# Key norms by one block-ones product, and small products set apart, in a hybrid RWKV-7 / sparse-attention layer

## The chip, the cores and the metric

The kernel runs on one core of one Trainium2 chip. The metric is device time in microseconds (us). Before the change the median of three runs is 1169.22 us (1169.16 to 1169.35). The profile is one more execution, taken by the hardware profiler.

## The reference

One decoder layer on 512 tokens of width 1024. A combined projection of the normalised input feeds two mixers, RWKV-7 time mixing and sparse attention; their outputs are gated, merged and projected, and a gated MLP with a causal convolution follows. All of it is float32. The change touches the RWKV-7 part:

```python
kk = heads(k * k_k)                       # 16 heads of 64 channels
kk = kk / jnp.maximum(jnp.sqrt(jnp.sum(kk * kk, axis=-1, keepdims=True)), 1e-12)
k = k * (1.0 + (a - 1.0) * k_a)
y = wkv7_scan(r, decay, k, v, -kk, kk * a)
mean = jnp.mean(y, axis=-1, keepdims=True)
var = jnp.mean(jnp.square(y - mean), axis=-1, keepdims=True)
y = ((y - mean) * lax.rsqrt(var + GN_EPS)) * ln_w + ln_b
y = (y + jnp.sum(r * k * r_k, axis=-1, keepdims=True) * v) * g
```

So the keys are divided by their norm in each head, the scan runs over time, and its output is normalised per head, scaled, shifted, joined by a bonus term and multiplied by a gate.

## The kernel before

**Layout.** Channels lie on the 128 partitions and the 512 tokens on the free axis. Sixteen heads make eight pairs, p = 0 to 7, in two groups of four. A projection of one block of 128 columns (`proj_steps`, L302) is 24 TensorE products of 128x512: each weight block is split into a high and a low part in a reduced-precision float32 format, and for each of eight k-tiles three products are made (L306, L307, L308). A product of two such parts is one pass; a product of two plain float32 operands shows as two records in the profile. The split (`split_w`) loads the raw weights, copies them to the high part on ScalarE (L124) and subtracts on GpSimd (L162); three buffers are turned for each of raw, high and low.

**Order.** The program is written as Python generators. `drive` takes one step of a filler (one k-tile of a projection, three products) and lets other generators, the threads, go on at given rates: a `yield` in a thread is a point where filler products come between. A scheduler then sets the order of each engine's instructions; `keep_in_program_order` pins some. Engines run their instructions in that order, and an instruction that waits holds up all those behind it on its engine.

**Stages of the RWKV part.** For each pair: `inputs` projects k, r and v and mixes each with its shifted self; `prep` makes the decay, the key norm and the scaled operands; `couple` makes the products between tokens of a chunk of 64 (L607), transposes (L140), and stores the bonus term (`bvd`, L642). For each group of four pairs, `invert` inverts the triangular blocks on VectorE, and `recur` first completes the inverses by small products of 32x32 (`mt` L705, `mm` L728) and then goes through eight chunks: state times operand (xw, L789), output (y, L760 and L753), solve (L805), state update (xs, L815). Between its chunks it collects the sums of the group norm (`stat1`, `stat2`). `finish` normalises, transposes back, applies ln_w and ln_b, adds the bonus and multiplies by the gate (L880, L881). The pairs 0 to 3 are prepared from 81 to 180 us; the first recurrence lies at 227 to 288 us, with the prep of pair 4 beside it; pairs 5 to 7 and the finish of the first group follow until 385 us; the second recurrence is at 437 to 488 us. From 488 us the scores of the sparse attention run, with the finish of the second group among them.

**The key norm.** In `prep`, Q holds the squares of the scaled keys, channels by tokens. Four products (`pn`, L541) with `sel`, a 128x2 matrix of ones and zeros, use pieces of Q as the stationary operand and give, for 128 tokens each, the sums of the two heads; the result has tokens on the partitions and eight columns. ScalarE takes the root (L543, with a table load ahead of it and one after it for the exponential), VectorE the maximum with 1e-12, a factor 2 and the reciprocal on 128x8. GpSimd spreads these to 128x512 (`nte`, L551; ScalarE L549 for pair 4), and four transposes (`pb`, L140) bring them back to channels by tokens in PSUM. From there VectorE multiplies them into KB (L570) and AR (L572).

**Other lines.** In `recur`, `stat1` subtracts the mean on GpSimd (L773) and squares on ScalarE (L775) right behind it. In `finish`, ScalarE applies ln_w and ln_b out of PSUM (L868, L871), GpSimd adds the loaded bonus (`bvl`, L857, L872), and VectorE multiplies by the gate product. At the end of the MLP, `post` multiplies the second half by its gain (L1363) and adds the two halves of the sum of squares (L1364) before the root and the reciprocal of the last norm.

## Time and profile before

| what | us |
|---|---|
| median of the runs | 1169.22 |
| the profiled execution's own time | 1171.52 |
| its span, first to last instruction | 1169.7 |
| TensorE busy (98%) | 1148.6 |
| VectorE busy (49%) | 574.0 |
| ScalarE busy (50%) | 579.5 |
| GpSimd busy (51%) | 595.2 |

Busy time of TensorE is the time in which at least one product is under way; neighbouring products overlap, so the spacing of their starts, not the duration of one, tells what a product costs. The page also gives the clock that the throttle granted to TensorE, and each view can be cut to a window. "Idle before" names what ended the wait of an engine.

### The profile page before, as it was taken

To read this page: it belongs to the slowest core of one execution; us is meant where nothing else is said; L and a number is where in the kernel's file an instruction comes from. 1 tells how busy PE (TensorE), PEld (TensorE's weight loads), DVE (VectorE), ACT (ScalarE), POOL (GpSimd) and SP (SyncE) were. 2 spreads that over 40 slices of the span, in tenths; PEclk is the share of its full clock that TensorE was granted. 3 is DMA by queue.
4 is the path that set the end of the run, shared out by engine and by line. 5 is a ranking of instruction groups with operands and counts; after the bars stand their busy time and mean duration, and the time that the engine had idled before them with its cause. 6 is when DMAs were issued, how large, how long until landed. Compare 5 with 4: busy or idle time off the path is not lost.

```text
span 1169.7 us, 19903 instructions
## 1 busy us (share of the span) xinstructions
PE 1148.6 (98%) x7418; PEld 927.3 (79%) x7418; DVE 574.0 (49%) x1196; ACT 579.5 (50%) x1149; POOL 595.2 (51%) x537
## 2 busy tenths in 40 slices
PE   9999999999999999999999999999999999999997
PEld 7888888867878887767677778889888888888886
DVE  4236555634456563587798735754443343331103
ACT  6446663534665334477576654534444444443311
POOL 4346654335666452497666635511565556554430
PEclk9999999989999999999999999999999999999999
DMA  7522335311443662225543136641233333334421
GB/s 245 134 65 75 103 99 167 96 64 53 113 125 93 188 198 92 91 60 145 170 149 97 46 97 181 209 156 39 80 99 99 97 94 99 99 97 136 127 64 72
DMA packets 95651, 131.95 MB, mean 113 GB/s; under 512 B 34177, under 2 KB 37057, under 8 KB 95298
## 3 DMA queue, kind: packets, MB, share of 16 engines
q1 hardware_dynamic: 79634, 116.26, 33.1%
q10 hardware_dynamic: 15920, 14.42, 3.9%
q8 instruction: 58, 0.95, 0.3%
q14 instruction: 39, 0.32, 0.1%
HBM read 108.30 MB, written 19.14 MB: 109 GB/s over the span
## 4 chain that ended last, share of the span: by engine, by line
PE 87%; DVE 4%; ACT 3%; POOL 2%; issue 1%; DMA 1%; SPq 0%; DVEq 0%; ACTq 0%; POOLq 0%
PE pu L223 6%; PE pu L221 6%; PE pu L222 6%; PE dn L1317 3%; PE dn L1316 3%; PE dn L1315 3%; PE o L1142 3%; PE pt L140 3%; PE ub L1199 3%; PE ub L1201 2%; PE ub L1200 2%; PE gt L306 2%; PE gt L308 2%; PE gt L307 2%; PE v L306 2%; PE v L308 2%
## 5 line engine op out<-in xcount | busy, mean ns | idle before, releaser
L1095 ACT ACTIVATE p<-p,stt 128x384 f32<-128x384 f32 (+3 forms) x128 | 70.7, 554 | 34.5 <-DVE stt L1093 32.9
L1069 POOL TENSOR_SCALAR p<-p,stt 128x512 f32<-128x512 f32 (+1 forms) x64 | 72.3, 1139 | 25.8 <-DVE stt L1064 15.5
L1457 DVE SCALAR_TENSOR_TENSOR u<-pu,cvec,u 128x511 f32<-128x511 f32 x44 | 33.0, 750 | 101.2 <-ACT u L1456 101.2
L1093 DVE CUSTOM_DVE_ANT_0 p<-s,rh 128x384 f32<-128x384 f32 (+3 forms) x128 | 59.0, 484 | 22.7 <-PE s L1079 18.3
L1463 DVE TENSOR_TENSOR al<-u,ah 128x512 fp32r<-128x512 f32 x22 | 23.8, 1080 | 45.4 <-ACT ah L1462 45.4
L140 PE MATMUL pt<-ident,p 128*128 128x128 f32 x320 | 44.3, 272 | 0.0
L1086 PE MATMUL s<-kst,qs 128*128 128x512 f32 (+1 forms) x128 | 39.2, 396 | 4.4 <-DVE stt L1093 4.1
L1461 POOL TENSOR_TENSOR u<-u,u 128x512 f32<-128x512 f32 x22 | 28.3, 1288 | 27.3 <-DVE u L1458 26.3
L1142 PE MATMUL o<-PT,vt 128*64 128x256 f32 (+3 forms) x256 | 41.5, 443 | 0.0
L140 PEld LDWEIGHTS pt<-ident,p 128*128 128x128 f32 x320 | 37.8, 141 | 4.4 <-issue 0.4
L1069 DVE TENSOR_SCALAR p<-p,stt 128x512 f32<-128x512 f32 (+1 forms) x64 | 35.3, 580 | 0.8
L1456 ACT ACTIVATE u<-pu,cvec 128x512 f32<-128x512 f32 x44 | 33.6, 764 | 3.0 <-PE pu L1419 3.0
L1458 DVE SCALAR_TENSOR_TENSOR u<-pu,cvec,u 128x510 f32<-128x510 f32 x44 | 33.0, 749 | 1.6
L1086 PEld LDWEIGHTS s<-kst,qs 128*128 128x128 f32 x128 | 20.9, 189 | 13.5 <-DVE stt L1093 9.3
L1142 PEld LDWEIGHTS o<-PT,vt 128*64 128x64 f32 x256 | 16.6, 136 | 18.8 <-issue 16.8
L1133 ACT ACTIVATE PT<-pt 128x512 f32<-128x512 f32 x48 | 27.3, 584 | 8.0 <-PE pt L140 7.8
L1363 DVE TENSOR_TENSOR p2tm<-dn,gb 128x512 f32<-128x512 f32 x4 | 2.8, 692 | 51.2 <-ACT p2jl L1361 51.2
L1135 DVE COPY PT<-pt 128x512 f32<-128x512 f32 x32 | 21.7, 678 | 8.4 <-PE pt L140 8.3
L1462 ACT ACTIVATE ah<-u 128x512 fp32r<-128x512 f32 x22 | 13.9, 633 | 22.0 <-POOL u L1461 22.0
L1095 ACT ACTIVATION_READ_ACCUMULATOR p<-p,stt 128x1 f32 x128 | 24.2, 189 | 0.0
L664 DVE TENSOR_TENSOR XP<-XP,TM 128x30 f32<-128x30 f32 (+14 forms) x60 | 20.3, 338 | 2.0
L162 POOL TENSOR_TENSOR up3l<-up30r,up3h 128x512 fp32r<-128x512 f32 x1 | 1.3, 1295 | 38.2 <-ACT up3h L124 38.2
(1755 smaller groups left out, 3953.8 us busy)
## 6 DMA issues: line engine op xcount, KB each, us to landing
gtd<-gt ACTq DMA_DIRECT2D x16, 256.0 KB, 2.2
qs<-qd SPq DMA_DIRECT2D x32, 128.0 KB, 3.3
g<-gtd SPq DMA_DIRECT2D x16, 256.0 KB, 3.2
xt<-in_x_dram SPq DMA_DIRECT2D x4, 512.0 KB, 5.5
bvd<-bv SPq DMA_DIRECT2D x8, 256.0 KB, 2.2
bvl<-bvd SPq DMA_DIRECT2D x8, 256.0 KB, 2.9
oad<-y SPq DMA_DIRECT2D x8, 256.0 KB, 2.5
kst<-kst ACTq DMA_DIRECT2D x16, 128.0 KB, 2.5
```

The source lines that it names most:

```text
L140: return te.transpose(o, i, ident)
L221: te.matmul(p, wh(k), mh(k), start=first and k == 0, stop=False)
L222: te.matmul(p, wh(k), ml(k), start=False, stop=False)
L223: te.matmul(p, wl(k), mh(k), start=False, stop=last and k == n - 1)
L306: te.matmul(p, wh(k), hh[:, k, :], start=k == 0, stop=False)
L308: te.matmul(p, wl(k), hh[:, k, :], start=False, stop=k == KT - 1)
L1069: (po if b else ve).tensor_scalar(o.pe[e, b, k], o.pe[e, b, k], st[e][:, 3, i:i + 1], None, op0=OP.mult)
L1086: m = te.matmul(s_[:, :n], qt, kt[:, x, b, :n], start=x == 0, stop=x == 1)
L1093: ve.tensor_tensor_reduce(sb, parts[b], rh[e][:, (3 - qb) * 128:], -1.0, BIG, OP.add, OP.min, st[e][:, 0, i:i + 1])
L1095: sc.activation(sb, sb, AF.Exp, scale=-1.0, bias=st[e][:, 0, i:i + 1], accum_out=st[e][:, 1, i:i + 1])
L1142: te.matmul(acc[e * 64:e * 64 + 64, j * 128:], vt[:, j, b * 256 + g * 64:b * 256 + g * 64 + 64], m[e][:, c:c + n], start=False, stop=k == ...
L1199: te.matmul(p, wh(k), sh[:, k, :], start=k == 0, stop=False)
```

## The change

The eight parts of the edit, and what each does:

1. **Key norm.** `pb` is now one float32 product of the 128x128 block matrix of ones (`onesr`, already there for the bonus term) with Q: each channel gets the sum of its head. Maximum with 1e-24, root and reciprocal then work in place on 128x512 in PSUM. The factors 2 and -2 become 0.5 and -1 in the two multiplications that read `pb`. The four `sel` products, the spreading and the four transposes are gone.
2. **Weight splits ahead.** While k is projected, the split of r's weights is issued after the sixth of eight k-tiles, and v's while r is projected.
3. **Two more yields in `couple`** ahead of the transposes of v and the products L607.
4. **Bunches in `recur`.** Two yields between each block of `mt` or `mm` products and its copies out of PSUM, so that the two blocks are apart; fewer yields after them. The inner products of y keep the program's order for the first seven chunks.
5. **Squares.** The squaring moves out of `stat1` to a later point of the next chunk, with two buffers.
6. **Finish.** The bonus is loaded straight into y2; VectorE applies ln_w and adds the bonus in one instruction out of PSUM, and adds ln_b as it multiplies by the gate. The ScalarE and GpSimd instructions for this are gone, the low part of g2 is split for 128 columns instead of 256, and the y2 buffers are two.
7. **Buffers.** `gates_` and one `plain_out` use the tag of y2 in place of that of `bvl`.
8. **Last norm.** The 128x1 addition goes ahead of the 128x512 multiplication.

How the order of the engines' instructions moves is shown at three places, of before and then of the change. A row has the line, the operation, output<-inputs and the size; xN counts equal rows that follow each other.

VectorE in the prep of pair 0. Before, from the norms (nt) to the operand AR:
```order
L544 TENSOR_SCALAR nt_918<-nt_918 128x8
L545 RECIPROCAL nt_918<-nt_918 128x8
L563 SCALAR_TENSOR_TENSOR Q_891<-K_643,vec,EC_924 128x512
L561 SCALAR_TENSOR_TENSOR A_937<-pa_901,EN_925 128x512
L565 TENSOR_TENSOR KB_936<-F_905,EN_925 128x8x64
L562 SCALAR_TENSOR_TENSOR A_937<-K_643,vec,A_937 128x512
L331 SCALAR_TENSOR_TENSOR K_874<-k_875,vec,K_874 128x511
L570 TENSOR_TENSOR KB_936<-pb_945,A_937 128x8x64
L572 SCALAR_TENSOR_TENSOR AR_859<-Q_891,pb_945 128x512
```

The change, from the maximum on the product pb to AR:
```order
L547 TENSOR_SCALAR pb_911<-pb_911 128x512
L559 SCALAR_TENSOR_TENSOR A_929<-pa_899,EN_917 128x512
L561 SCALAR_TENSOR_TENSOR Q_889<-K_641,vec,EC_916 128x512
L560 SCALAR_TENSOR_TENSOR A_929<-K_641,vec,A_929 128x512
L563 TENSOR_TENSOR KB_928<-F_903,EN_917 128x8x64
L549 RECIPROCAL pb_911<-pb_911 128x512
L332 SCALAR_TENSOR_TENSOR K_872<-k_873,vec,K_872 128x511
L565 SCALAR_TENSOR_TENSOR KB_928<-pb_911,A_929 128x8x64
L568 SCALAR_TENSOR_TENSOR AR_857<-Q_889,pb_911 128x512
```
The reciprocal is now 128x512 and stands four instructions further back, next ahead of K, KB and AR; KB (L563) stands ahead of it.

TensorE where the first recurrence begins (mt and mm are the products that complete the inverses, gt a projection that fills). Before, around mt and then around mm:
```order
L307 MATMUL gt_2323<-hl,gt04h_2324 128x512
L308 MATMUL gt_2323<-hh,gt04l_2325 128x512
L705 MATMUL mt_2365<-x_2126 32x32 x32
L705 MATMUL mt_2400<-x_2126 32x32 x32
L306 MATMUL gt_2323<-hh,gt04h_2330 128x512
L307 MATMUL gt_2323<-hl,gt04h_2330 128x512
...
L308 MATMUL gt_2323<-hh,gt04l_2331 128x512
L728 MATMUL mm_2455<-TT_870,x_2126 32x32 x32
L140 MATMUL pb_2564<-ident,nte_2354 128x128 x3
L728 MATMUL mm_2490<-TT_870,x_2126 32x32 x32
L140 MATMUL pb_2564<-ident,nte_2354 128x128
L805 MATMUL xw_2552<-LV_869,TT_870 64x64 x4
L805 MATMUL xs_2553<-LV_869,TT_870 64x64 x2
```

The change:
```order
L308 MATMUL gt_2277<-hh,gt04l_2279 128x512
L703 MATMUL mt_2313<-x_2092 32x32 x32
L306 MATMUL gt_2277<-hh,gt04h_2284 128x512
...
L308 MATMUL gt_2277<-hh,gt04l_2285 128x512
L703 MATMUL mt_2354<-x_2092 32x32 x32
L306 MATMUL gt_2277<-hh,gt04h_2284 128x512
...
L308 MATMUL gt_2406<-hh,gt14l_2408 128x512
L306 MATMUL gt_2406<-hh,gt14h_2413 128x512
L727 MATMUL mm_2422<-TT_868,x_2092 32x32 x32
L727 MATMUL mm_2463<-TT_868,x_2092 32x32 x32
L307 MATMUL gt_2406<-hl,gt14h_2413 128x512
```
Six filler products part the two mt blocks, and nineteen stand between mt and mm; the two mm blocks still follow each other, and the transposes into pb are gone.

ScalarE in the first recurrence (UV copies out of xs, YT out of y, SQ squares, v0h high parts of weights). Before, chunks 3 and 4:
```order
L775 ACTIVATE SQ_2755<-YT_2525 128x512
L810 ACTIVATE UV_868<-xs_2725 64x4x64
L764 ACTIVATE YT_2525<-y_2602 128x4x64
L764 ACTIVATE YT_2525<-y_2603 128x4x64
L810 ACTIVATE UV_868<-xs_2786 64x4x64
L124 ACTIVATE v0h_3016<-v01r 128x512
```

The change, chunks 2 to 4:
```order
L814 ACTIVATE UV_866<-xs_2619 64x4x64
L124 ACTIVATE v0h_2863<-v01r 128x512
L779 ACTIVATE SQ_2732<-YT_2511 128x512
L814 ACTIVATE UV_866<-xs_2677 64x4x64
L766 ACTIVATE YT_2511<-y_2554 128x4x64
L766 ACTIVATE YT_2511<-y_2555 128x4x64
L814 ACTIVATE UV_866<-xs_2738 64x4x64
```
The square still stands directly ahead of the UV copy of chunk 3 (in the change xs_2677, before xs_2725); the copies of weights around it moved.

```diff
@@ -299,13 +299,15 @@
...
 
-    def proj_steps(blk, name, p):
-        wh, wl = split_w(a["wf"][blk], name)
+    def proj_steps(blk, name, p, w=None, ahead=None):
+        wh, wl = w or split_w(a["wf"][blk], name)
         wh, wl = wslice(wh), wslice(wl)
...
             te.matmul(p, wl(k), hh[:, k, :], start=False, stop=k == KT - 1)
+            if ahead is not None and k == 5:
+                ahead()
             yield
...
@@ -486,18 +487,23 @@
...
     def inputs(p, o):
+        w = {}
+
+        def ahead(x):
+            w[x] = split_w(a["wf"]["rkv".index(x) + 3 + 3 * p], f"{x}{p}")
+
         K = o.K = rw.tile([128, S], F32, tag="K", name=f"K{p}", bufs=2)
         pk = pj(f"k{p}")
-        yield from proj_steps(4 + 3 * p, f"k{p}", pk)
+        yield from proj_steps(4 + 3 * p, f"k{p}", pk, None, lambda: ahead("r"))
         shift(pk, K, 8 + p)
...
         pr = pj(f"r{p}")
-        yield from proj_steps(3 + 3 * p, f"r{p}", pr)
+        yield from proj_steps(3 + 3 * p, f"r{p}", pr, w["r"], lambda: ahead("v"))
         shift(pr, R, p)
...
         pv = pj(f"v{p}")
-        yield from proj_steps(5 + 3 * p, f"v{p}", pv)
+        yield from proj_steps(5 + 3 * p, f"v{p}", pv, w["v"])
         shift(pv, VW[:, 64:], 16 + p)
...
@@ -536,19 +542,11 @@
...
         yield
-        pn = (pz if p == GP else py)(f"pn{p}")
-        for t in range(4):
-            te.matmul(pn[:, 2 * t:2 * t + 2], Q[:, t * 128:(t + 1) * 128], sel, start=True, stop=True)
-        nt = rw.tile([128, 8], F32, tag="nt", name=f"nt{p}", bufs=2)
-        sc.activation(nt, pn[:, :8], AF.Sqrt)
-        ve.tensor_scalar(nt, nt, 1e-12, 2.0, op0=OP.max, op1=OP.mult)
-        ve.reciprocal(nt, nt)
-        nte = rw.tile([128, 8, 64], F32, tag="T", name=f"nte{p}", bufs=NT)
-        nb = nt[:, :, None].to_broadcast([128, 8, 64])
-        if p == GP:
-            sc.activation(nte, nb, AF.Copy)
-        else:
-            po.tensor_copy(nte, nb)
+        pb = pz(f"pb{p}")
+        te.matmul(pb, onesr.bitcast(F32), Q, start=True, stop=True)
+        ve.tensor_scalar(pb, pb, 1e-24, None, op0=OP.max)
+        sc.activation(pb, pb, AF.Sqrt)
+        ve.reciprocal(pb, pb)
         EC = rw.tile([128, 8, 65], F32, tag="EC", name=f"EC{p}", bufs=1)
...
@@ -564,12 +562,10 @@
...
         yield
-        pb = pz(f"pb{p}")
-        for t in range(4):
-            tr(pb[:, t * 128:(t + 1) * 128], nte[:, 2 * t:2 * t + 2].rearrange("p a b -> p (a b)"), ident)
-        ve.tensor_tensor(KB[:, :, 0, :], pb.rearrange(c8, t=64), A.rearrange(c8, t=64), op=OP.mult)
+        ve.scalar_tensor_tensor(KB[:, :, 0, :], pb.rearrange(c8, t=64), 0.5, A.rearrange(c8, t=64), op0=OP.mult,
+                                op1=OP.mult)
         o.Q = None if gr else Q
-        ve.scalar_tensor_tensor(gr.AR[p % GP][:, 0, :] if gr else Q, Q, -2.0, pb, op0=OP.mult, op1=OP.mult)
+        ve.scalar_tensor_tensor(gr.AR[p % GP][:, 0, :] if gr else Q, Q, -1.0, pb, op0=OP.mult, op1=OP.mult)
         tc.keep_in_program_order(ve.scalar_tensor_tensor(F, R, vec[:, V_RK + p:V_RK + p + 1], F, op0=OP.mult,
...
@@ -588,6 +584,8 @@
...
         sc.activation(gr.Dc[:, i], EC[:, :, 64], AF.Copy)
+        yield
+        yield
         yield
...
@@ -706,6 +704,8 @@
...
                             tc.keep_in_program_order(m)
+            yield
+            yield
             for h in range(2):
...
@@ -716,8 +716,7 @@
...
             behind(sc.activation(gr.diag[0][lo, :, 0:32], gr.diag[1][lo], AF.Copy))
-        for _ in range(4):
-            yield
+        yield
         for q in range(GP // 2):
...
@@ -727,6 +726,8 @@
...
                                   stop=True)
+            yield
+            yield
             for h in range(2):
...
@@ -734,8 +735,7 @@
...
         YT = gr.YT = rh_.tile([128, 4, GP, 2, 64], F32, tag="XB", name=f"YT{g}", bufs=2)
-        for _ in range(3):
-            yield
+        yield
         hs = [slice(0, 64), slice(64, 128)]
...
@@ -757,8 +757,10 @@
...
                 for i in range(GP):
-                    te.matmul(y[h][hs[(c + i) % 2], i], gr.GS[:, 1 + i, c, h, :], gr.UV[:, c, i, h, :],
-                              start=c == 0, stop=c == 0 or i >= 2)
+                    m = te.matmul(y[h][hs[(c + i) % 2], i], gr.GS[:, 1 + i, c, h, :], gr.UV[:, c, i, h, :],
+                                  start=c == 0, stop=c == 0 or i >= 2)
+                    if c < 7:
+                        tc.keep_in_program_order(m)
             if c % 2:
...
@@ -771,8 +773,10 @@
...
             po.tensor_tensor(Y8, Y8, st[:, 0, a, :, None].to_broadcast([128, 2 * GP, 64]), op=OP.subtract)
-            sq[a] = rh_.tile([128, 2 * GP, 64], F32, tag="TB", name=f"SQ{g}{a}", bufs=1)
-            sc.activation(sq[a], Y8, AF.Square)
+
+        def square(a):
+            sq[a] = rh_.tile([128, 2 * GP, 64], F32, tag="TB", name=f"SQ{g}{a}", bufs=2)
+            sc.activation(sq[a], YT[:, a].rearrange("p i h v -> p (i h) v"), AF.Square)
 
...
@@ -821,11 +825,15 @@
...
                 St = SN
+                if c >= 3 and c % 2:
+                    square((c - 3) // 2)
                 yield
...
                 inner(c)
+        square(2)
         stat2(2, free)
         stat1(3, free)
+        square(3)
 
...
@@ -849,36 +857,38 @@
...
             gh = rh_.tile([128, 256], F32R, tag="gh", name=f"gh{p}", bufs=1)
-            gl = rh_.tile([128, 256], F32R, tag="gl", name=f"gl{p}", bufs=1)
-            split_to(a["g2"][p], gh, gl, f"g2{p}", 256, p=rh_, late=True, tag="TM", bufs=1)
-            po.tensor_copy(gh[64:96, 128:], gl[64:96, 128:].bitcast(F32))
-            yield
-            bvl = rh_.tile([128, S], F32, tag="bvl", name=f"bvl{p}", bufs=1)
-            tc.keep_in_program_order(sy.dma_start(bvl, bvd[p]))
+            gl = rh_.tile([128, 128], F32R, tag="gl", name=f"gl{p}", bufs=1)
+            raw = rh_.tile([128, 256], F32, tag="TM", name=f"g2{p}r", bufs=1)
+            sy.dma_start(raw, a["g2"][p])
+            tc.keep_in_program_order(sc.activation(gh, raw, AF.Copy))
+            po.tensor_tensor(gl, raw[:, :128], gh[:, :128].bitcast(F32), op=OP.subtract)
+            gx = gh[64:96, 128:]
+            po.tensor_tensor(gx, raw[64:96, 128:], gx.bitcast(F32), op=OP.subtract)
+            yield
+            y2 = rh_.tile([128, S], F32, tag="TB", name=f"y2{p}", bufs=2)
+            tc.keep_in_program_order(sy.dma_start(y2, bvd[p]))
             yield
...
                 tr(pt[:, t * 128:(t + 1) * 128], Y8[:, t].rearrange("p h v -> p (h v)"), ident)
-            y2 = rh_.tile([128, S], F32, tag="TB", name=f"y2{p}", bufs=1)
             y2v = y2.rearrange("p (t s u) -> p t s u", s=2, u=64)
...
             if i % 2 == 0:
-                sc.activation(y2, pt, AF.Identity, scale=lnw, bias=lnb)
+                ve.scalar_tensor_tensor(y2, pt, lnw, y2, op0=OP.mult, op1=OP.add)
             else:
                 for x in range(2):
-                    sc.activation(y2v[:, :, x], ptv[:, :, 1 - x], AF.Identity, scale=lnw, bias=lnb)
-            po.tensor_tensor(y2, y2, bvl, op=OP.add)
+                    ve.scalar_tensor_tensor(y2v[:, :, x], ptv[:, :, 1 - x], lnw, y2v[:, :, x], op0=OP.mult, op1=OP.add)
             yield
...
             te.matmul(pg, gh[:, :128], lg1l, start=False, stop=False)
-            te.matmul(pg, gl[:, :128], lg1h, start=False, stop=False)
+            te.matmul(pg, gl, lg1h, start=False, stop=False)
             te.matmul(pg, gh[:96, 128:], lg2, start=False, stop=True)
-            ve.tensor_tensor(y2, y2, pg, op=OP.mult)
+            ve.scalar_tensor_tensor(y2, y2, lnb, pg, op0=OP.add, op1=OP.mult)
             sy.dma_start(oad[p], y2)
...
@@ -1360,8 +1370,8 @@
...
         tm = p.tile([128, 512], F32, tag=name + "tm", name=f"{name}tm{t}", bufs=3)
+        ve.tensor_tensor(ss[:, 2:3], ss[:, 0:1], ss[:, 1:2], op=OP.add)
         ve.tensor_tensor(tm, acc, gb[:, 512:], op=OP.mult)
-        ve.tensor_tensor(ss[:, 2:3], ss[:, 0:1], ss[:, 1:2], op=OP.add)
         r = rstd_of(ss[:, 2:3], D, f"{name}r{t}", p)
...
```

## The prediction, written before the result

> **What bounds the kernel now.** I read the page's first parts, then the view of TensorE's waits, then windows and timelines of the stages that the change touches.

> The page's busy line, and its chain of waits by engine:
> ```profile
> PE 1148.6 (98%) x7418; PEld 927.3 (79%) x7418; DVE 574.0 (49%) x1196; ACT 579.5 (50%) x1149; POOL 595.2 (51%) x537
> ...
> PE 87%; DVE 4%; ACT 3%; POOL 2%; issue 1%; DMA 1%; SPq 0%; DVEq 0%; ACTq 0%; POOLq 0%
> ```
> TensorE is busy for 98% of the span and holds 87% of the chain; the others are half idle. So time goes only where TensorE issues less, waits less, or runs at a better clock. Its waits (the columns are us in total, times, longest):
> ```profile
> PE s L1086 <- DVE stt L1093: 4.1, 7, 1.3
> PE xs L815 <- ACT UV L810: 2.3, 4, 0.8
> ...
> PE s L1079 <- DVE y L881: 1.3, 1, 1.3
> ...
> PE pg L880 <- POOL gh L854: 0.9, 1, 0.9
> PE r L308 <- POOL r6l L162: 0.6, 1, 0.6
> ```
> The clock is seen in windows (length, busy time of PE, PEld, DVE, ACT, POOL with instructions, granted clock, DMA share, GB/s):
> ```profile
> 229.80:233.20 3.40, 3.40 (x44) 2.85 (x39) 1.47 (x3) 3.32 (x5) 0.00 (x0) 0.50 0.02 5
> ...
> 240.06:246.86 6.80, 6.80 (x20) 4.17 (x18) 2.35 (x4) 1.16 (x4) 4.18 (x3) 0.50 0.38 118
> ...
> 441.45:444.75 3.30, 3.30 (x9) 2.57 (x8) 0.70 (x1) 3.26 (x3) 0.00 (x0) 0.50 0.02 6
> ...
> 488.00:560.00 72.00, 68.58 (x393) 50.60 (x389) 58.50 (x190) 53.09 (x146) 57.61 (x62) 1.00 0.39 110
> ```
> Both recurrences begin with a stretch in which TensorE is busy throughout and has half its clock; elsewhere the clock is nearly full.

> **The change part by part.** All terms are TensorE time.

> *Products of the key norm.* TensorE in the prep of pair 0 (start, duration):
> ```profile
> 83.16 0.40 PE L308 MATMUL k<-hh,k1l 128*128 128x512 f32 x1
> 83.39 0.95 PE L541 MATMUL pn<-sel,Q 128*128 128x2 f32 x8
> 84.21 0.48 PE L306 MATMUL k<-hh,k1h 128*128 128x512 f32 x1
> 84.53 0.40 PE L307 MATMUL k<-hl,k1h 128*128 128x512 f32 x1
> ...
> 87.03 0.60 PE L140 MATMUL pb<-ident,nte 128*128 128x128 f32 x4
> 87.39 0.48 PE L306 MATMUL k<-hh,k1h 128*128 128x512 f32 x1
> ...
> 91.11 0.39 PE L307 MATMUL r<-hl,r1h 128*128 128x512 f32 x1
> 91.49 0.50 PE L308 MATMUL r<-hh,r1l 128*128 128x512 f32 x1
> 91.82 1.04 PE L140 MATMUL pv<-ident,V 128*128 128x128 f32 x8
> 92.61 0.47 PE L306 MATMUL r<-hh,r1h 128*128 128x512 f32 x1
> 93.02 2.06 PE L607 MATMUL g<-AR,KB 64*128 64x128 f32 x32
> ```
> A projection product costs the spacing of starts, 0.23 us, and 0.32 just behind other products (84.21 to 84.53), 0.09 more. The `pn` products take 84.21 − 83.39 = 0.82, the `pb` transposes 0.36, and each is followed by the 0.09: 1.36 us a pair go. What comes is one plain float32 product over 512 columns. The trace has one row of that kind at full clock, with one row of weights:
> ```profile
> 4.94 1.98 PE L119 MATMUL gb<-g1r 1*128 1x512 f32 x4
> ```
> Two products in 1.98 us, less some 0.16 of latency (a projection product lasts 0.39 and is spaced 0.23): 0.91 each. The bounds are 0.46 (two passes at 0.23) and 0.99 (1.98 / 2). With 0.91 + 0.09, a pair saves 0.36; times seven (pair 4 lies in the recurrence, below): **2.5 us**, bounds 2.0 to 5.7.

> *Couple and splits ahead.* Today one projection product stands between `pv` and `g` and costs 0.41 in place of 0.23; the transposes of v and `g` now follow each other: 0.18. The second weight part of r came late (91.11 to 91.49 is 0.38, 0.15 over the spacing); with the split issued earlier this goes. 0.33 for six pairs is **1.8 us** with something off for pairs where r was not late; bounds 0.5 to 2.0.

> *The chain behind the norm.* Root and maximum on 512 columns are covered by neighbours (`pa` on ScalarE 0.65, AR on VectorE 0.67). The reciprocal is the unknown, and I price it by width:
> ```profile
> L1063 DVE RECIPROCAL stt<-stt 128x4 f32<-128x4 f32 x32 | 5.5, 173 | 5.4 <-ACT p L1095 5.1
> ...
> L835 DVE RECIPROCAL gst<-gst 128x32 f32<-128x32 f32 x2 | 0.7, 346 | 1.5 <-ACT gst L834 1.5
> ...
> L180 DVE RECIPROCAL n1r<-n1r 128x1 f32<-128x1 f32 x4 | 0.7, 164 | 3.1 <-ACT n1r L124 3.1
> ```
> (346 − 164) / 31 = 5.9 ns a column, so 512 columns cost 0.16 + 3.0 = 3.2 us. The rows of one and four columns give slopes down to 3 ns (1.7 us); from four to 32 columns it is 6.2 ns (3.3 us). VectorE has room, 574 of 1170 us busy; the question is whether TensorE reaches `g` first. Rows of the chain for pair 0:
> ```profile
> 83.01 0.78 ACT L537 ACTIVATE F<-pa,vd 128x512 f32<-128x512 f32 x1
> 83.81 1.28 ACT L543 ACT_TABLE_LOAD   x1
> ```
> ```profile
> 83.17 1.22 DVE L531 TENSOR_TENSOR_SCAN C<-rmask,T 128x512 f32<-128x512 f32 x1 [0.76 <-POOL T L530]
> ...
> 88.53 1.09 DVE L565 TENSOR_TENSOR KB<-F,EN 128x512 f32<-128x512 f32 x1
> ...
> 91.46 0.67 DVE L572 SCALAR_TENSOR_TENSOR AR<-Q,pb 128x512 f32<-128x512 f32 x1
> ```
> The scan ends at 84.39. In the new order both exponentials come ahead of the root: EC to 85.0, EN to 85.6, Dc and a weight copy to 86.4, the table load 1.28, the root 0.65: 88.3. VectorE has done maximum, A, Q, A and KB by about 88.7; reciprocal to 91.8, then K, KB, AR at 0.6 to 0.7 each: 93.7. TensorE reaches `g` three k-tiles later than today: 93.02 + 2.07 (nine products) − 0.36 − 0.33 = 94.4, and I take 94.2 to have 0.2 in hand. **Slack 0.45 us** in the pairs whose ScalarE order is like this one (0, 2, 6); in 1, 3, 5 and 7 the root stands ahead of EN, and I work out 1.0 or more. So it is hidden, at 0, as long as the reciprocal stays under some 3.65 us.

> *First recurrence.* TensorE there:
> ```profile
> 227.04 3.80 PE L705 MATMUL mt<-x 32*32 32x32 f32 x128
> ...
> 238.33 0.68 PE L805 MATMUL xw<-LV,TT 64*64 64x64 f32 x8 [0.41 <-DVE TT L735]
> 239.87 0.51 PE L805 MATMUL xs<-LV,TT 64*64 64x64 f32 x4 [0.86 <-DVE TT L735]
> ```
> The half clock comes behind 32x32 products without a gap and again behind the `mm` products and the 1.27 us of waits; half-clock time is 3.4 + 6.8 us by the windows; half of it, 5.1, is lost. The new order puts six projection products between the two `mt` blocks and nineteen ahead of `mm`, so no stretch of small products is over 2.4 us. Against it: the TT copies now stand behind the 4.06 us ScalarE copy of XL, a table load (1.28) and two weight copies, which I work out to 2.1 us of waits at L809 in place of 1.27, and two or three more changes between kinds of product (0.1 each), and the reciprocal for pair 4 sits ahead of VectorE's `mt` copies but ends before `mm` needs them. 5.1 − 0.8 − 0.6 = **3.7 us**; bounds −1.4 (clock as before) to 5.1.

> [...]

> *Second recurrence.*
> ```profile
> 441.06 0.50 PE L306 MATMUL q<-hh,q1h 128*128 128x512 f32 x1
> ...
> 444.76 0.44 PE L306 MATMUL q<-hh,q2h 128*128 128x512 f32 x1
> ```
> Nine products of q start from 441.06 to 444.33, and the tenth at 444.76: 3.70 us in place of 0.32 + 8 × 0.23 = 2.2, so 1.5 comes back, less four more changes at 0.1: **1.1 us**, bounds −0.4 to 1.5.

> *Inside the chunks.* The 2.3 us at L815 come from this: the copy UV that TensorE wants stands behind the square on ScalarE, which waits for GpSimd.
> ```profile
> 261.34 0.63 ACT L775 ACTIVATE SQ<-YT 128x512 f32<-128x512 f32 x1 [3.95 <-POOL YT L773]
> 261.88 0.36 ACT L810 ACTIVATE UV<-xs 64x256 f32<-64x256 f32 x1
> ```
> The square was moved in the program, but in the new ScalarE order it still stands just ahead of the UV copy of chunks 3 and 5, and now 7. I put this at **0**, bounds −1.0 (two new waits at 0.5) to 2.3.

> *Finish.* Of the waits for GpSimd (0.9 for `gh`, 0.6 for r6l), whose queue loses the y additions and half the split, I count **0.8**, bounds 0 to 1.5. In exchange VectorE takes about 0.7 us for each of four pairs, 2.8, inside the score stage, where it is busy 58.5 of 72 us and TensorE waits on it (L1093), and the order has ten projection products (2.3) less there to cover. TensorE idles 3.4 us against VectorE's 13.5, a quarter; a quarter of 5.1 is **1.3 us lost**, bounds −1.3 (the wait at L881 goes) to 5.1.

> *Tail.* The root now waits for no 128x512 multiplication:
> ```profile
> 1163.94 0.69 DVE L1363 TENSOR_TENSOR p2tm<-dn,gb 128x512 f32<-128x512 f32 x1 [2.70 <-ACT p2jl L1361]
> ...
> 1164.73 0.30 ACT L124 ACTIVATE p2r<-p2ss,vec 128x1 f32<-128x1 f32 x1 [0.82 <-DVE p2ss L1364]
> ```
> Addition first, root (0.3) under the multiplication; the reciprocal follows it: **0.45**, bounds 0.3 to 0.6.

> Sum: 2.5 + 1.8 + 3.7 + 1.1 + 0 + 0.8 − 1.3 + 0.45 = 9.05 us. The profiled execution took 1171.52 with a span of 1169.7, 1.82 around it, and is 2.3 over the median of 1169.22. Its span becomes 1160.7, its own time 1162.5, the median **1160.2 us**.

> **The rivals.**

> 1. *The half clock stays.* In the new order the two `mm` blocks still follow each other (2.4 us), and behind them come 64x64 products with up to 2.1 us of waits, much like the stretch ahead of 240.06. For it: that stretch. Against: fillers now stand on both sides. If the first recurrence gains nothing of its clock and the second its 1.1, it is 1160.2 + 5.1 = 1165.3. [...]

> 2. *A steeper reciprocal.* If the slope over 512 columns is a third higher, 8.3 ns, the reciprocal takes 4.4 us and `g` waits 4.4 − 3.65 = 0.75 in three pairs and 0.2 in four: 3.05 lost, 1163.3. For it: the slope rises from 3 ns (one to four columns) to 6.2 (four to 32), and 32 columns are far from 512; against it: no row is over 6.2. [...]

> 3. *The other side: the norm is in front of `g`.* If the reciprocal, read from and written to PSUM, costs twice the slope, 6.5 us, `g` waits at all seven places: 3 × (3.3 − 0.45) + 4 × (3.3 − 1.0) = 17.8 lost; 1160.2 + 17.8 = **1178.0**, slower. It decides from 3.65 us on and cancels the gain of 9 at about 5.3 (3 × 1.65 + 4 × 1.1). For it: no row here shows a reciprocal in PSUM. Against: AR reads PSUM at 0.67, as other multiplications read SBUF.

> 4. *The score stage is VectorE's.* Then all 5.1 us come back there: 3.8 more than I charge, 1164.0. For it: 4.1 us of waits on L1093. Against: VectorE idles 13.5 us there.

> 5. *More than forecast.* The new product costs two passes (3.2 more) and the chunk waits go after all (2.3): about 1154.7.

> **How the numbers follow.** This kernel's measurement tells about 0.2%, 2.3 us, from no change: faster means under 1166.9. Forecast 0.50 (its own range 1157 to 1163.5), half clock 0.17, steeper reciprocal 0.10, reciprocal in front 0.07, score stage 0.09, more 0.07. Faster: 0.50 + 0.07 + 0.10 + 0.12 of the half clock + 0.05 of the score stage = 0.84; same: 0.05 + 0.03 = 0.08; slower: 0.07 + 0.01 = 0.08. The range runs from the fifth case to just over the first: 1154.5 to 1167.

> **What would show it.** Right: `pb` spaced near 0.91; the reciprocal at 3.2 us on 128x512; no wait at `g` over 0.3; granted clock above 0.9 in both openings; waits at xs from UV near 2.3 still; VectorE busier by 3 us in the score stage with TensorE's idle there near 4.7. Wrong: a `g` waiting on AR or KB in every pair, a half-clock stretch of 3 us or more behind `mm`, or TensorE idle over 7 us in the score stage.

## The result: slower, by the chain ahead of `g` and by the bunches

The change takes 1183.70 us (median of four runs, 1181.73 to 1183.83), the kernel before 1169.28 on the same chip: ratio 1.0115, 95% interval 1.0099 to 1.0131. Forecast were 1160.2 us and a range of 1154.5 to 1167. The profiled execution of the change is the one of 1181.73, span 1179.8, which is 10.1 over the span of before. The medians are 14.4 us apart; the profiled execution of before lay about 2 us over its median and that of the change about 2 us under, so the traces show 10 of the 14.

The page's busy line and the chain of waits by engine, of the change:
```profile
PE 1147.6 (97%) x7338; PEld 921.9 (78%) x7338; DVE 612.6 (52%) x1208; ACT 575.3 (49%) x1136; POOL 575.0 (49%) x522
...
PE 84%; DVE 10%; ACT 2%; POOL 2%; issue 1%; DMA 0%; DVEq 0%; POOLq 0%; ACTq 0%
```
TensorE is busy 1.0 us less than before, and the span is 10.1 longer: the loss is TensorE standing idle (time at half clock, a granted clock of 0.50 in the windows, is 13.7 us in both executions without the first and last 20 us; half of it is counted as lost below, an estimate: 1.7 us for a stretch of 3.41). VectorE's share of the chain went from 4 to 10%. TensorE's waits in the change (us in total, times, longest):
```profile
PE g L605 <- DVE AR L568: 6.6, 5, 3.0
PE xs L819 <- ACT UV L814: 3.6, 5, 0.9
PE v L306 <- DVE K L332: 3.0, 2, 1.6
PE y L760 <- ACT UV L814: 1.9, 2, 1.3
...
PE pct L140 <- POOL sc L1055: 1.3, 1, 1.3
PE vtp L140 <- ACT vt L1018: 1.2, 1, 1.2
...
PE s L1096 <- DVE stt L1103: 0.9, 3, 0.5
```
`g` waits 6.6 us where it waited 0.3, v's projection waits 3.0 for VectorE to read k out of PSUM, the copies UV cost 5.5 in place of 2.3; the softmax (L1103) costs less than the 4.1 of before.

Where the time went, by stage. For each milestone on TensorE (first product of `g` of pair 0, first `mt`, first state update, and so on) I took its time less 0.228 us for every projection product issued ahead of it (the spacing of their starts at full clock: 1.82 us for eight, 165.69 to 167.51 in the change), so that fillers moved from one stage to another do not count, and subtracted the same for before. The table gives what each stage adds to that difference, in us; it is worked out from the timelines. "End" is the last product of the kernel. Names of runs are those of the experiments below, whose medians come from sittings in which before itself had 1169.28 to 1171.54; ratios are to the before of the same sitting; "g0" is the part up to the first `g`, which lies between -0.5 and 1.9 and is mostly scatter between executions; h3 is before in another execution.

| run | g0 | preps 0-3 | opening 1 | chunks 1, couple 4 | preps 5-7 to opening 2 | opening 2 | chunks 2 | scores to end | sum |
|---|---|---|---|---|---|---|---|---|---|
| change | 0.1 | 4.5 | -2.8 | 2.7 | 4.2 | -0.9 | 1.1 | 1.9 | 10.6 |
| e1 | 1.1 | 3.9 | -5.2 | -3.3 | 3.6 | -1.1 | 0.0 | 0.0 | -1.1 |
| e2 | 1.5 | -0.7 | -0.7 | 2.6 | 0.1 | -0.9 | 1.1 | 2.0 | 4.9 |
| e3 | 0.5 | -0.4 | -5.7 | 1.0 | -0.5 | -0.9 | 1.1 | 1.8 | -3.1 |
| e4 | 0.3 | 4.5 | -3.9 | -0.7 | 4.2 | -0.9 | -1.6 | 6.9 | 8.7 |
| f1 | -0.2 | -1.8 | -6.8 | 2.6 | 0.5 | -0.9 | 1.1 | 2.0 | -3.4 |
| f2 | 0.2 | 3.5 | -5.3 | 0.3 | 1.8 | 0.0 | 0.0 | 0.0 | 0.4 |
| f3 | 1.9 | 4.5 | -2.8 | 2.5 | 8.3 | -0.9 | 1.1 | 4.9 | 19.4 |
| f4 | 0.0 | 0.1 | -1.1 | 1.0 | 0.4 | -0.9 | -0.6 | 0.7 | -0.5 |
| g1 | 1.6 | -1.8 | -6.8 | -2.5 | -0.9 | -0.9 | -1.6 | 5.2 | -7.7 |
| g2 | 1.8 | 8.1 | -4.0 | 1.0 | 6.4 | -0.9 | 1.1 | 2.0 | 15.5 |
| g3 | -0.5 | -1.8 | -6.6 | 1.2 | -0.9 | -0.4 | -0.2 | -3.3 | -12.5 |
| g4 | 1.6 | -1.8 | -6.8 | 0.9 | -0.9 | -0.9 | -0.6 | -3.2 | -11.6 |
| h1 | 1.6 | -1.8 | -6.6 | -2.2 | -0.9 | -0.2 | -1.9 | -1.9 | -14.0 |
| h2 | 1.9 | 4.5 | -5.6 | 1.0 | 4.2 | 0.0 | -0.2 | -3.3 | 2.6 |
| h3 | 0.2 | 0.1 | -1.5 | 0.0 | 0.2 | -0.8 | 0.0 | 0.1 | -1.7 |

The preps lost 8.7 where 4.3 were to be gained, both openings gained nearly what was forecast, the chunks lost 3.8 and the score stage 1.9. The largest piece is pair 3. TensorE there, and then VectorE and GpSimd (start, duration):
```profile
167.74 1.04 PE L140 MATMUL pv<-ident,V 128*128 128x128 f32 x8
171.74 2.59 PE L605 MATMUL g<-AR,KB 64*128 64x128 f32 x32 [2.97 <-DVE AR L568]
174.26 0.79 PE L306 MATMUL gt<-hh,gt01h 128*128 128x512 f32 x1
```
```profile
159.00 1.23 DVE L537 TENSOR_TENSOR_SCAN C<-rmask,T 128x512 f32<-128x512 f32 x1 [1.95 <-POOL T L536]
...
161.78 1.68 DVE L561 SCALAR_TENSOR_TENSOR Q<-K,vec,EC 128x512 f32<-128x512 f32 x1
163.38 3.35 DVE L549 RECIPROCAL pb<-pb 128x512 f32<-128x512 f32 x1
166.65 0.67 DVE L559 SCALAR_TENSOR_TENSOR A<-pa,EN 128x512 f32<-128x512 f32 x1
...
168.45 1.82 DVE L560 SCALAR_TENSOR_TENSOR A<-K,vec,A 128x512 f32<-128x512 f32 x1
170.31 0.69 DVE L565 SCALAR_TENSOR_TENSOR KB<-pb,A 128x512 f32<-128x512 f32 x1
170.92 0.68 DVE L568 SCALAR_TENSOR_TENSOR AR<-Q,pb 128x512 f32<-128x512 f32 x1
```
```profile
161.27 1.64 POOL L585 TENSOR_TENSOR AR<-R,EC 128x512 f32<-128x512 f32 x1
...
168.46 1.26 POOL L162 TENSOR_TENSOR gt11l<-gt110r,gt11h 128x512 fp32r<-128x512 f32 x1 [0.48 <-ACT gt11h L124]
```
From the scan to AR VectorE has no gap, 12.6 us. In before it was 9.5 (157.01 to 166.55), with 1.9 us of gaps in it:
```profile
157.01 1.23 DVE L531 TENSOR_TENSOR_SCAN C<-rmask,T 128x512 f32<-128x512 f32 x1 [0.76 <-POOL T L530]
...
161.09 0.75 DVE L563 SCALAR_TENSOR_TENSOR Q<-K,vec,EC 128x512 f32<-128x512 f32 x1 [1.54 <-ACT EC L555]
...
163.38 1.78 DVE L562 SCALAR_TENSOR_TENSOR A<-K,vec,A 128x512 f32<-128x512 f32 x1
...
165.87 0.68 DVE L572 SCALAR_TENSOR_TENSOR AR<-Q,pb 128x512 f32<-128x512 f32 x1
```
The reciprocal took the 3.35 us that it was priced at (3.2). Q and A (L560), 0.75 us in most pairs of before, last 1.68 and 1.82 here, beside a GpSimd instruction, and both end 0.55 us behind its end; A is at 1.75 to 1.82 in all eight pairs of the change. Behind the 2.97 us of waiting the clock falls as well: the products of gt behind `g` are 0.43 apart again (175.28, 175.71 in the timeline), in this window of the change:
```profile
173.10:176.48 3.38, 3.38 (x18) 2.76 (x16) 2.94 (x5) 0.93 (x2) 2.57 (x3) 0.50 0.41 155
```
In pair 1 the wait is not at `g` but at the next pair's v, which is written where k was. VectorE frees that place with K, and K stands behind the reciprocal (113.45 to 116.80) and the long A. VectorE, then TensorE:
```profile
119.58 0.74 DVE L332 SCALAR_TENSOR_TENSOR K<-k,vec,K 128x511 f32<-128x511 f32 x1
```
```profile
120.47 0.47 PE L306 MATMUL v<-hh,v2h 128*128 128x512 f32 x1 [1.63 <-DVE K L332]
```

### The profile page after: what moved, and what is told of

Its sections match the earlier page's. It is cut to its first block, busy times and chain, and to the rows that moved or that the text cites. A ratio compares the mean times of both kernels' runs of the same rounds, so it can differ in the third digit from the quotient of the medians.

```text
span 1179.8 us, 19692 instructions
## 1 busy us (share of the span) xinstructions
PE 1147.6 (97%) x7338; PEld 921.9 (78%) x7338; DVE 612.6 (52%) x1208; ACT 575.3 (49%) x1136; POOL 575.0 (49%) x522
## 4 chain that ended last, share of the span: by engine, by line
PE 84%; DVE 10%; ACT 2%; POOL 2%; issue 1%; DMA 0%; DVEq 0%; POOLq 0%; ACTq 0%
PE pu L221 6%; PE pu L222 6%; PE pu L223 6%; PE dn L1327 3%; PE dn L1325 3%; PE dn L1326 3%; PE o L1152 3%; PE pt L140 3%; PE ub L1209 3%; PE ub L1211 2%; PE ub L1210 2%; PE gt L307 2%; PE gt L306 2%; DVE pb L549 2%; PE v L306 2%; PE gt L308 2%
## 5 line engine op out<-in xcount | busy, mean ns | idle before, releaser
L1079 POOL TENSOR_SCALAR p<-p,stt 128x512 f32<-128x512 f32 (+1 forms) x64 | 72.4, 1142 | 29.6 <-DVE stt L1074 14.5
L1103 DVE CUSTOM_DVE_ANT_0 p<-s,rh 128x384 f32<-128x384 f32 (+3 forms) x128 | 59.3, 484 | 23.1 <-PE s L1089 16.9
L140 PE MATMUL pt<-ident,p 128*128 128x128 f32 x320 | 44.1, 273 | 0.5 <-POOL p L1079 0.5
L140 PEld LDWEIGHTS pt<-ident,p 128*128 128x128 f32 x320 | 37.5, 141 | 5.5 <-ACT PT L1143 0.8
L1079 DVE TENSOR_SCALAR p<-p,stt 128x512 f32<-128x512 f32 (+1 forms) x64 | 34.7, 571 | 0.6
L549 DVE RECIPROCAL pb<-pb 128x512 f32<-128x512 f32 x8 | 26.8, 3353 | 0.0
L639 DVE TENSOR_TENSOR bv<-pbo,V 128x512 f32<-128x512 f32 x8 | 5.5, 692 | 38.6 <-PE pbo L637 38.6
L605 PE MATMUL g<-AR,KB 64*128 64x128 f32 x256 | 18.6, 295 | 6.6 <-DVE AR L568 6.6
L610 POOL TENSOR_TENSOR KB<-KB,EC 128x512 f32<-128x512 f32 x16 | 19.3, 1220 | 10.8 <-PE g L605 9.1
```

Of the source, the lines that this page charges most:

```text
L140: return te.transpose(o, i, ident)
L549: ve.reciprocal(pb, pb)
L1079: (po if b else ve).tensor_scalar(o.pe[e, b, k], o.pe[e, b, k], st[e][:, 3, i:i + 1], None, op0=OP.mult)
L1103: ve.tensor_tensor_reduce(sb, parts[b], rh[e][:, (3 - qb) * 128:], -1.0, BIG, OP.add, OP.min, st[e][:, 0, i:i + 1])
```

## The experiments

**e1, the key norm alone**, on the kernel before:
```diff
+pb = pz(f"pb{p}"); te.matmul(pb, onesr.bitcast(F32), Q, ...)
+max, Sqrt, reciprocal on pb        # and 0.5, -1.0 in KB, AR
-pn, nt, nte, transposes into pb
```

> The kernel before with the new key norm alone (part 1 of the change). Theory A (the norm chain on VectorE, with a reciprocal of 3.35 us on 128x512 in its midst, is in front of TensorE in the preps): the time rises to between 1176 and 1182 us, with at least 6 us of TensorE waiting at g for AR or at a projection for K. Rival B (the other parts, splits ahead and yields, made the preps late): 1165 to 1170 us, as the products alone save.

1170.51 against 1171.17, ratio 0.9998 (0.9987 to 1.0009). The value is near B's, the reason is not: the preps lose 7.5, as theory A has it (5.0 us of waits for AR and K, and 3.7 at `g` that the profile puts down to GpSimd), but the rest gains 9.6: no half clock in either opening of this execution, and in the new ScalarE order two squares of the first recurrence stand behind the UV copy. So theory A is right on the stage and wrong on the sum.

**e2, the change with the old norm.**

> The changed kernel with the old key norm put back (pn, 128x8 root and reciprocal, spreading, transposes); all else is the change. Theory A: the loss of the preps goes, about 9 us off the changed kernel's 1183.7, so 1172 to 1176; what is left over the 1169.3 of before is the chunks and the score stage. Rival B: still 1180 or more.

1177.13, ratio to before 1.0051 (1.0033 to 1.0068): 6.6 less than the change. The loss of the preps is gone (-0.7 and 0.1). What remains is in the chunks (3.7) and the scores (2.0).

**e3, the change without the reciprocal.** The root is multiplied in its place, so the keys are not divided by their norm.
```diff
-ve.tensor_scalar(pb, pb, 1e-24, None, op0=OP.max)
+ve.tensor_scalar(pb, pb, 1e-24, 1e-3, op0=OP.max, op1=OP.mult)
-ve.reciprocal(pb, pb)
```

> The changed kernel without the reciprocal on 128x512: the maximum takes a factor 0.001 in its second operation, the root follows, and KB and AR are multiplied by that root; so the keys are not divided by their norm, and all other work stays. Theory A: the waits at g and K go, 6 to 9 us off 1183.7: 1174 to 1178. Rival C (the root with its two table loads and its place on ScalarE is what is late, not the reciprocal): under 3 us off, 1181 or more.

1167.81, ratio 0.9972 (0.9962 to 0.9983), 15.9 under the change. Rival C falls. The gain is larger than the waits, since the half-clock stretches went too (three in the change between 20 and 1160 us, none here).

**e4, the square pinned** to its place in the program:
```diff
-sc.activation(sq[a], ..., AF.Square)
+tc.keep_in_program_order(sc.activation(sq[a], ..., AF.Square))
```

> The changed kernel with the square pinned to its place in the program, so that on ScalarE the UV copy of chunks 3, 5 and 7 stands ahead of the square and no longer behind it. Theory A (the square, waiting for GpSimd's subtraction, holds up the copy that TensorE wants): the waits of xs and y for UV fall from 5.5 us to under 2, and the time by 3 to 4 us, to about 1180. Rival D (the copies are late because y is pinned or for their own operands): under 1 us.

1180.14, ratio to before 1.0080 (1.0061 to 1.0099): 3.6 less than the change. The waits for UV fell from 5.5 to 0.7 us. The two recurrences gained 3.4 and 2.7 by the stage table, and the scores gave 5.0 back, in waits for GpSimd and one half-clock stretch.

**f1, logarithm and exponential** in place of root and reciprocal, all computed:
```diff
-sc.activation(pb, pb, AF.Sqrt)
-ve.reciprocal(pb, pb)
+sc.activation(pb, pb, AF.Ln)
...
 sc.activation(EN, C, AF.Exp, scale=-1.0)
+sc.activation(pb, pb, AF.Exp, scale=-0.5)
```

> The changed kernel with the root and the reciprocal replaced on ScalarE: the logarithm of the maximum, and behind EN the exponential with the factor -0.5, both 128x512 in PSUM; two table loads a pair as before, and no reciprocal on VectorE. All is computed. Theory A (what costs in the preps is the reciprocal's 3.35 us in VectorE's queue): as without the reciprocal, 1167 to 1171. Rival C (the late root and its tables on ScalarE): 1179 or more, since ScalarE now has 0.6 us more in the same chain.

1168.14, ratio 0.9979 (0.9967 to 0.9991): 15.6 under the change, as e3. The groups of f1 that took the place of the reciprocal's 26.8 us of VectorE time:
```profile
L548 ACT ACTIVATE pb<-pb 128x512 f32<-128x512 f32 x8 | 4.7, 582 | 0.1
...
L554 ACT ACTIVATE pb<-pb 128x512 f32<-128x512 f32 x8 | 4.6, 580 | 0.0
```
The added work on ScalarE does not show in the time; the place in VectorE's queue was the cost, with the half clock that followed its waits (0.50 from 173.08 and from 388.12 in the change, each behind 2.97 us of waiting at `g`).

**f2, the norm alone with logarithm and exponential.**

> The kernel before with the new product for the norm and with logarithm and exponential in place of root and reciprocal; no other part of the change. Theory A: the norm alone (e1, 1170.5) less the 8 us that the reciprocal costs in its preps: 1162 to 1165, faster than both kernels. Rival E (the norm alone came out even for another reason, since its recurrence had no half clock and better placed squares): the preps lose nothing, but the recurrence is again that of before, 1167 to 1170.

1171.52, ratio 1.0016 (1.0003 to 1.0028): theory A missed by 7. Rival E falls too: the preps lose 5.3, and the first opening gains 5.3. The waits of f2:
```profile
PE g L596 <- DVE AR L561: 7.7, 6, 2.2
```
Without the two yields of `couple`, TensorE is at `g` about three k-tiles (2 us) sooner, and the chain is late even without a reciprocal. So a free VectorE alone is not enough; f1, which has the other parts of the change as well, has no long wait at `g`. That the yields are what it takes of them is likely, but no run has them alone.

**f3, the change with the old finish** (and the buffers of before for y2, the square and `gates_`).

> The changed kernel with the finish of before (ln_w and ln_b on ScalarE, bonus by GpSimd, one buffer for y2 and the square); all else is the change. Theory F (the finish on VectorE and its loss of cover cost what the score stage lost, 1.9 us): 1181 to 1182. Rival G (the finish gains elsewhere what it loses there): 1183 to 1185; rival H (the score stage is later for another reason): no change within 0.7 us.

1189.90, ratio 1.0170 (1.0151 to 1.0190): 6.2 slower than the change; none of the three values. The new finish is a gain: 4.1 beside the preps of 5 to 7 (where f3 has one more double stretch of half clock, 3.4 us) and 3.0 in the score stage.

**f4, the bunches alone**, on the kernel before (two yields behind each block of mt and mm, fewer later).

> The kernel before with the yields of the recurrence's opening alone (blocks of mt and mm apart). If small products without a gap cost the clock, the half-clock stretches at both openings go: 3 to 5 us less, 1164 to 1166. Rival I (half clock falls on whole stretches of 3.4 us by a grid of the chip's own, and whether an opening is hit depends on where the grid lies, as in the norm alone, whose unparted blocks kept the full clock): within 2 us of before, and half-clock stretches still there in some form.

1170.94, ratio 1.0005 (0.9996 to 1.0015): no change, as rival I. Behind `mt` there is no half clock in either opening; behind `mm` of the first it is still there, 6.8 us, beside 2.0 us of waits in place of 1.3.

**g1, f1 with the square pinned.**

> The changed kernel with logarithm and exponential (f1, 1168.1) and the square pinned behind the UV copy (e4). In e4 the two recurrences became 6 us shorter and the score stage 5 us longer. If the score stage's loss there hung on a half clock and on where the trace happened to lie: 1163 to 1165 here, faster than both kernels by 4 us or more. Rival: what the recurrences gain comes back as waits for GpSimd in the score stage: 1167 to 1169.

1164.03, ratio 0.9943 (0.9922 to 0.9964). As the first theory has it, though the rival has a part: the recurrences gain 7.8 over f1 (1.7 of it a half-clock stretch that f1 has at 277.88), and the scores give 3.2 back.

**g2, the change with three more yields ahead of `g`.**

> The changed kernel, reciprocal and all, with three more yields ahead of the transposes of v and g, so that TensorE reaches g some three to five k-tiles later in every pair. Theory A (g simply comes too early for VectorE's chain): the 9.6 us of waits at g for AR and at v for K fall under 4 and the time by 4 to 8 us, to 1176 to 1180. Rival J (VectorE as a whole is late in the preps, and a later g makes the next steps late by as much): under 2 us off, the waits move to v for K or to the next stage.

1188.24, ratio 1.0145 (1.0126 to 1.0164): 4.5 slower than the change, so the first theory falls and the rival was still too mild. `g` and v's projection wait 9.4 us in sum, as much as before the yields. The next pair's v waits for the PSUM of k, which VectorE frees with K (L332) from behind the reciprocal. VectorE's load from `g` of pair 0 to that of pair 3, in the windows of before, of the change and of g2:
```profile
93.02:166.60 73.58, 73.43 (x510) 61.19 (x509) 40.74 (x60) 46.83 (x79) 45.28 (x43) 1.00 0.34 91
```
```profile
94.90:171.74 76.84, 72.02 (x481) 58.70 (x481) 56.86 (x60) 49.24 (x78) 42.01 (x39) 1.00 0.31 89
```
```profile
100.08:175.86 75.78, 70.69 (x466) 56.83 (x466) 54.16 (x58) 47.65 (x76) 40.68 (x38) 0.98 0.31 84
```
From 41 us VectorE rose to 57 and 54 in about the same time; three to four reciprocals are 10 to 13 of the 16 that were added. By the table the preps lose 5.8 more than in the change; 1.7 of it is one more half-clock stretch, behind the wait of pair 1 (from 123.15), and most of the rest was not traced.

**g3, f1 without the bunches.**

> The changed kernel with logarithm and exponential (f1) without the yields that part the mt and mm blocks. If parting them keeps the clock at the openings: half-clock stretches of 3.4 us come back there, 2 to 5 us slower than f1, 1170 to 1173. Rival I (the grid of the clock decides, not the parting): within 1.5 us of f1's 1168.1.

1159.81, ratio 0.9907 (0.9884 to 0.9929): 8.3 faster than f1, the other way than both theories. The first opening keeps its full clock with unparted blocks; the second has a stretch of half clock behind `mt`, from 431.59.

**g4, f1 with y not pinned.**

> The changed kernel with logarithm and exponential (f1) without the pin that keeps the inner products of y in the program's order. The scheduler then sets the square behind the UV copy in two of six places in a recurrence pair more than in f1. Theory: fewer waits of xs and y for UV (5.5 us in f1), 1 to 3 us faster, 1165 to 1167. Rival: the y products split in pieces among others cost as much, within 1 us of 1168.1.

1160.55, ratio 0.9913 (0.9893 to 0.9934): 7.6 faster than f1, far over the estimate. The chunks give 3.4 of it (1.7 is again f1's half-clock stretch), the scores 5.2.

**h1, g3 with the square pinned.**

> The changed kernel with logarithm and exponential, without the bunches (g3, 1159.8) and with the square pinned behind the UV copy (4.9 us of waits for UV in g3). Theory: the waits go and are not given back where the score stage has its cover: 1155 to 1157. Rival: as with the pin in f1 and e4, half or more comes back in the score stage: 1158 to 1161.

1157.32, ratio 0.9878 (0.9856 to 0.9899): the fastest here, 1.2% under before. The waits for UV are gone; 1.4 of the 5.1 that the chunks gain come back in the score stage.

**h2, the change without the bunches.**

> The changed kernel, reciprocal and all, without the yields that part mt and mm. Theory K (the bunches take projection products away that the score stage needs, 5 us, whatever stands in the preps): 1175 to 1180. Rival: the eight us between f1 and g3 came from a half clock in f1 and not from the bunches; then 1182 to 1185.

1172.71, ratio 1.0015 (1.0002 to 1.0027): 11.0 faster than the change. Theory K holds and is too small: by the table 5.2 in the scores, 2.9 in the chunks (most of it half clock that reaches into chunks 1 in the change), 1.9 in both openings. The score stage's first 70 us, of the change and of h2 (PE, PEld, DVE, ACT, POOL, clock, DMA, GB/s):
```profile
500.04:570.00 69.96, 64.56 (x350) 45.57 (x350) 56.88 (x187) 48.16 (x134) 50.25 (x55) 1.00 0.35 104
```
```profile
495.04:565.00 69.96, 66.29 (x380) 49.25 (x381) 60.73 (x196) 50.68 (x142) 54.11 (x59) 1.00 0.42 122
```
TensorE idles 5.4 us in the one and 3.7 in the other, and h2 gets 30 TensorE instructions more done. Of the 1440 projection products 1323 were issued ahead of the first score in the change, 1314 in h2, 1313 in before. All runs with 1320 or more lose 1.8 to 6.9 us in this stage, the others lose at most 0.7 and gain up to 3.3. It takes two parts for such a number, the bunches and the pin of y: without the bunches (g3, h1, h2) it is 1314, with the bunches but without the pin (f4, g4) 1315.

**h3, before again**, for its clock.

> The kernel before, unchanged, profiled once more, for where its half clock falls. Grid theory: stretches of 3.4 us again, but not all at the same places (the first ends at another time), and the span differs by about 1.7 us for each one more or less. Rival (the work at the openings alone decides): again 229.8 to 233.2, 240.0 to 246.9 and 441.4 to 444.8 within 0.5 us.

1169.88, one run. Half clock in two stretches, behind `mt` again and behind `mm` for 3.4 us in place of 6.8; none in the second recurrence. In the windows of h3:
```profile
230.40:233.75 3.35, 3.35 (x32) 2.75 (x28) 1.42 (x3) 3.27 (x5) 0.00 (x0) 0.50 0.02 5
240.63:244.00 3.37, 3.37 (x9) 2.22 (x10) 2.09 (x3) 0.63 (x1) 3.37 (x3) 0.50 0.35 86
...
436.40:450.40 14.00, 13.63 (x300) 11.30 (x299) 3.79 (x6) 8.42 (x10) 3.79 (x3) 1.00 0.40 128
```
The work is that of before and its blocks are unparted; yet the second opening has the full clock here and is 0.8 us shorter. The half-clock stretches of an execution begin on one grid of 3.413 us, as read from their starts (last section), so each follows one window of that grid. The windows ahead, cut to `mt` alone (the first number behind the length is its busy time on TensorE), in before, both followed by half clock:
```profile
226.40:229.81 3.41, 2.77 (x99) 2.77 (x101) 0.12 (x1) 0.59 (x1) 1.00 0.02 5
438.03:441.44 3.41, 3.10 (x110) 2.93 (x104) 0.70 (x1) 0.85 (x2) 1.00 0.44 133
```
In h3, the first followed by half clock, the other two, which share the second opening's `mt`, not:
```profile
226.96:230.37 3.41, 3.03 (x108) 3.04 (x110) 0.38 (x1) 0.59 (x1) 1.00 0.02 5
435.17:438.58 3.41, 2.17 (x78) 2.18 (x80) 0.00 (x0) 0.14 (x1) 1.00 0.68 239
438.58:442.00 3.42, 1.62 (x58) 1.46 (x52) 1.39 (x2) 1.03 (x2) 1.00 0.32 81
```

## Why the prediction was wrong, step by step

- **Products of the norm and couple** (4.3 forecast): where the chain is not late (g1, g3, h1), preps gain 1.8 and 0.9, 2.7 in all. The first group's 1.8, for the three pairs behind the first `g`, is near the forecast (2.0); e2, with the old norm, has 0.7 of it. In the second group 0.9 came in place of 2.0, and why is open. The new product took 0.86 (83.88 to 84.97 in the timeline, less one projection product): the price of 0.91 was right.
- **The chain behind the norm** (0 forecast) is the step that failed. Its price for the reciprocal was right, 3.35 against 3.2; that is 6.2 ns a column, (3.35 − 0.16) / 511, and no run shows the 8.3 of the second rival. The slack was wrong: 0.45 us for pairs like 0, "1.0 or more" for the others. The long waits are in the preps of exactly the other pairs, 1, 3, 5 and 7: 1.6 (at the next v), 3.0, 1.4 (at v) and 3.0 us. I worked pair 0 through from its rows and gave the others a number from the place of the root alone. In pair 3 VectorE is never idle from scan to AR: the 1.9 us of gaps of before are filled, and the chain is still 3.1 longer. Two neighbours of the reciprocal take 1 us more each beside GpSimd, as A of pair 3 in before already showed (1.78). I also left out that K, which frees the PSUM of the next k for the next v, stands behind it. Measured against g1: 4.5 + 1.8 in the first group, 4.2 + 0.9 in the second, 11.4 us in place of 0, with some 3.4 of it half clock behind the two long waits. The third rival named the place and the sign (1178); its condition, a reciprocal over 3.65 us, was not needed.
- **Openings** (3.7 and 1.1 forecast): 2.8 and 0.9 came; against the other execution of before (h3) it is about 1.4 and 0.1. Behind `mt` the traces agree with the reason. In the seven executions with unparted blocks (before, h3, e1, f2, g3, h1, h2) half clock follows `mt` in eight of fourteen openings, just those in which `mt` takes 2.77 us or more of one window of the grid; where two windows share it, with 2.51 or less in each, the clock stays full, so by these windows e1, g3, h1 and h2 owe the full clock of their first opening to where the grid happened to lie. In the ten with parted blocks no window holds over 2.0 us of `mt`, and none of the twenty openings has half clock behind it. Behind `mm` the reason fell, and the first rival was right: the change has 6.8 us of half clock there (from 248.18), as before had. It goes with TensorE's waits from `mm` to the first state update: 1.1 to 2.0 us in the seven executions that have it (before, h3, the change, e2, e4, f3, f4), at most 0.8 in the others, but for g2 (2.0, at full clock). With the reciprocal the waits are 0.5 where the blocks are unparted (e1, h2) and 2.0 in the change, priced at 2.1; with logarithm and exponential there are none. All this is read across the traces; no run was made to test it.
- **Chunks** (0, bounds -1.0 to 2.3): 3.8 lost. The reading of the order was right, a square ahead of UV at one more place in each recurrence, but the waits for UV rose by 3.2 and not by 1.0 at most. Some 1.7 of the loss is no wait for UV: 3.9 us of the half clock behind `mm` fall into chunks 1, and e3, g2 and h2, which have none there, lose 1.0 in place of 2.7. In h2 and g3 one square of the second recurrence stands behind UV, so the bunches have a share in that order; so has the pin of y (g4).
- **Finish** (net 0.5 lost): the finish itself gains 6.2 (f3, which has 3.4 of it from one more double stretch of half clock). The lost cover was charged to the finish at a quarter; it belongs to the bunches together with the pin of y, which use the fillers up sooner (1320 to 1323 ahead of the first score with both, 1314 or 1315 with either undone), and costs 5.2 (h2, g4). The 0.8 counted for waits on GpSimd did not come in the second group: where before waited 0.6 and 0.9 for it, g1 waits 1.5 at `pg` for ScalarE's `gh` (317.12).
- **Tail** (0.45): from the last product to the end of the span it is 6.4 us after (1179.8 − 1173.38) and 7.0 before (1169.7 − 1162.73), about 0.6. Over all runs it is 6.4 to 6.9 with the new order and 6.8 to 7.0 with the old, 0.3 on average: right in size.

Shown: the reciprocal's place in VectorE's queue (e2, e3, f1), the square ahead of UV (e4, g1, h1), the bunches together with the pin of y (g3 and h2 without the one, g4 without the other, with nearly the same gain), the finish (f3). Not settled: why the waits behind `mm` are shorter under the new norm, why a pinned square sends part of its gain into waits for GpSimd in the score stage, and why the bunches and the pin of y cost cover only together.

## What to carry to other kernels

Work out the slack of a lengthened chain at its worst place, with the queue of its engine summed over all instructions and at the durations that they have beside another engine; a price that is right for the instruction says nothing of the room for it. When the order is a scheduler's, test each part in the company it will have: bunches that cost nothing alone (f4) cost 11 us in the change (h2), and a norm that cost nothing alone (e1) cost 15 us in the change by its reciprocal (f1). Filler work is a stock: what an early stage uses, a later stage lacks.
